# Dilated attention on one core: head pairs' products in runs, values stationary, one softmax scale, last group's values first

## The chip, the core and the metric

The kernel runs on one core of a Trainium2 chip. The metric is device time in microseconds (us), the median of three timed runs. A core has a matrix engine (TensorE, PE in the profile), a vector engine (VectorE, DVE), a scalar engine (ScalarE, ACT), a general engine (GpSimd, POOL), and a queue from which its transfers are issued (SyncE, SP). Each engine takes its own instructions in the order in which the program holds them, and waits on semaphores for the others.

## The reference, cut to what matters

Two layers act on 256 tokens of width 1024. Each is a gated feed-forward block, a mixer and another gated block, with RMS norms around each. The first layer's mixer is a convolution with a state-space part (the hybrid stage), the second's is the dilated attention that is changed here:

```python
qkv = (u @ w_qkv).reshape(bsz, seq, 3, ATTN_GROUPS, ATTN_HEADS, ATTN_HEAD_DIM)   # 3 groups, 8 heads, 64
for g, (window, dilation) in enumerate(DILATED_PATTERNS):
    o, l = dilated_window_attention(qkv[:, :, 0, g], qkv[:, :, 1, g], qkv[:, :, 2, g], slopes, window, dilation)
    outs.append(o)
    lses.append(l)
weights = jax.nn.softmax(jnp.stack(lses, axis=0), axis=0)
merged = jnp.einsum('gblh,gblhd->blhd', weights, jnp.stack(outs, axis=0).astype(jnp.float32))
return merged.reshape(bsz, seq, ATTN_OUT_WIDTH).astype(u.dtype) @ w_o
```

So there are three groups of eight heads, each with its own mask and its own softmax. The weighting over the groups by their log sums is the same as one softmax over the keys of all three groups together, and both kernels compute it in that way.

## The kernel before, in words

All activations stay on the chip; 178 weight units of 1 MB come in from memory. A product in nearly full f32 precision is made of three products of a rounded part (names `wh`, or `h`) and a rest (`wl`, or `l`). A weight unit lands in `raw`; ScalarE writes its rounded part `wh` and VectorE the rest `wl` in pieces of 128x1024 (`split`, `prefetch`). For units 38 to 55, those of the hybrid stage, GpSimd makes `wl` in pieces of 128x256. There are four slots each for `raw`, `wh` and `wl`.

The code does not fix the order of the instructions. Its functions record operations (`Recorder.add`), and `schedule` then places them: each engine takes, among the operations that could start at about the same estimated time, the one with the lowest rank, which is the order of recording with an offset from `moved`. The estimates come from `cost` and `latency`, and slots of buffers are given out in the same pass. All instructions are issued from line 423, so rows of the trace are told apart by tile names. `a`, `w`, `t` and `c` are PSUM banks (4, 2, 1 and 1 of them); `s` are the large SBUF slots (18), `cv`, `v`, `y` and `g` smaller kinds, `m` small columns, `x` the transposed input, `ident` the unit matrix.

Before the stage, the feed-forward stage hands over each half of the tokens (t = 0 and 1, 128 each) in turn: its last sums are normed and transposed into `x` (`_post_pre`, `to_transposed`). The attention stage is `attention`, line 1103:

- `values([0, 1])` multiplies the input by the value weights of groups 0 and 1, 24 matmuls for each token half and group, into a `w` bank (names `w<-wh,x`), and ScalarE copies the result to a `v` tile.
- For each group, `proj` makes q and then k, transposed (features on partitions), in `by_parts`: 16 matmuls into a `w` bank (names `w<-x,wh` and `w<-x,wl`), a ScalarE copy of one half, and a VectorE sum into a `cv` tile. One tile holds the four heads of two blocks; the even head of a pair lies on partitions 0 to 63, the odd one on 64 to 127.
- `softmax(g)` makes the scores. Half t = 0 has 128 keys and eight narrow products (64x128 by 64x128), half 1 has 256 keys and eight wide ones. They go to `a` banks. VectorE adds the mask table times the head's slope and takes the maxima, ScalarE exponentiates with the sums accumulated. From the second group on, the maximum is the running one, and factors `old` rescale the sums so far.
- `weigh(g)`, one group later, transposes the probabilities (72 transposes over all groups, into `t` and `c`), ScalarE copies them to `s` tiles, and 72 products with the probabilities stationary (128x128) and 64 columns of values moving give the weighted values, in an `a` bank. VectorE rescales the running sum `num` by `old` and adds.
- `values([2])` comes ahead of the last `weigh`. Then the sum is divided by the denominator, transposed (8 transposes), split, and multiplied by the output weights (48 matmuls, `a<-wh,x`), and the next stage's handover follows.

## Time and profile before

| | |
|---|---|
| timed runs | 1129.19, 1132.75, 1132.56 us; median 1132.56 |
| the profiled execution's own time | 1132.12 us, its span 1130.3 |
| TensorE busy | 1095.5 us of the span |
| VectorE, ScalarE, GpSimd busy | 738.6, 635.2, 148.2 us |
| granted TensorE clock, mean | 0.993 |
| attention stage on TensorE | 772.7 to 934.3 us of the span |
| hybrid stage | about 225 to 396 us |

The profile is of one execution. A row of a group of instructions reads: line, engine, operation, output <- inputs, partitions x elements, count, then busy time, mean length of one in ns, and idle time before them with what ended it. A row of the timeline begins with its start and length in us. A row of the sums by stretch gives the stretch, its length, and the busy time and number of instructions of PE, its weight loads, DVE, ACT and POOL, then granted clock, DMA share and GB/s. Matmuls overlap, so the time of a run is read from its start to the start of what follows; an f32 matmul leaves two records (two passes), each with a weight load of its own.

### The profile page before, as it was taken

What the parts mean: (1) busy time and instruction counts of PE and PEld (TensorE: products, weight loads), DVE (VectorE), ACT (ScalarE), POOL (GpSimd) and SP (SyncE); (2) the same over time, 40 slices, a digit from 0 to 9 for tenths busy, and PEclk for the clock granted to TensorE, in tenths of its full rate; (3) what the DMA queues carried; (4) which work ended last, traced back from release to release, by engine and by line L of the source; (5) the groups of instructions that cost most, each with busy time, mean ns of one, the idle gap of its engine ahead of it and who ended that gap; (6) DMA issues with size and microseconds to landing.
All of it is one profiled execution on the core that took longest, in us unless ns stands there. A gap on an engine that the chain in (4) does not pass through costs nothing.

```text
span 1130.3 us, 15336 instructions
## 1 busy us (share of the span) xinstructions
PE 1095.5 (97%) x5830; PEld 919.5 (81%) x5830; DVE 738.6 (65%) x1248; ACT 635.2 (56%) x1217; POOL 148.2 (13%) x200
## 2 busy tenths in 40 slices
PE   6999999999899999999999999999999999999997
PEld 5888888798767778888878888888877877888885
DVE  5756556799797685655686555667575657555563
ACT  7645545788667564554565454545565456455452
POOL 0000000379795300000010000001000000000000
PEclk9999999999999999999999999999999999999999
DMA  9755454534333466546546546554632424654521
GB/s 349 260 189 186 165 208 149 190 146 150 112 109 116 186 229 217 186 157 215 186 149 224 205 174 221 180 193 159 237 138 79 150 75 152 220 181 174 215 83 38
DMA packets 30203, 196.55 MB, mean 174 GB/s; under 512 B 3633, under 2 KB 4529, under 8 KB 7601
## 3 DMA queue, kind: packets, MB, share of 16 engines
q1 hardware_dynamic: 30128, 195.57, 48.9%
q8 instruction: 45, 0.74, 0.2%
q14 instruction: 30, 0.24, 0.1%
HBM read 194.51 MB, written 1.05 MB: 173 GB/s over the span
## 4 chain that ended last, share of the span: by engine, by line
PE 63%; DVE 4%; ACT 3%; POOL 3%; issue 1%; DVEq 0%; POOLq 0%; ACTq 0%
PE w L423 26%; PE a L423 22%; PE t L423 8%; PE c L423 7%; ACT s L423 1%; POOL wl L423 1%; ACT wh L423 1%; DVE y L423 1%; POOL s L423 1%; DVE wl L423 1%; DVE s L423 1%; POOL m L423 1%; DVE h L423 1%; DVE x L423 0%; DVE m L423 0%
## 5 line engine op out<-in xcount | busy, mean ns | idle before, releaser
L423 DVE TENSOR_TENSOR wl<-raw,wh 128x1024 fp32r<-128x1024 f32 (+1 forms) x322 | 385.1, 1220 | 215.6 <-ACT wh L423 214.0
L423 ACT ACTIVATE wh<-raw 128x1024 fp32r<-128x1024 f32 (+2 forms) x466 | 375.7, 854 | 232.4 <-PE a L423 91.5
L423 PE MATMUL w<-x,wh 128*128 128x512 f32 (+1 forms) x992 | 315.6, 373 | 3.5 <-DVE cv L423 2.1
L423 PE MATMUL w<-x,wl 128*128 128x256 f32 x880 | 247.9, 282 | 0.0
L423 PE MATMUL a<-wh,s 128*128 128x512 f32 x768 | 246.2, 395 | 0.0
L423 PEld LDWEIGHTS w<-x,wh 128*128 128x128 f32 x992 | 179.8, 189 | 40.2 <-DVE cv L423 3.1
L423 PEld LDWEIGHTS a<-wh,s 128*128 128x128 f32 x768 | 143.9, 188 | 34.7 <-DVE s L423 0.6
L423 PEld LDWEIGHTS w<-x,wl 128*128 128x128 f32 x880 | 166.9, 190 | 1.9 <-issue 0.6
L423 PE MATMUL w<-wh,x 128*128 128x512 f32 x480 | 159.3, 405 | 2.5 <-ACT x L423 2.5
L423 PE MATMUL a<-wl,s 128*128 128x512 f32 x384 | 151.8, 395 | 1.8 <-POOL wl L423 1.8
L423 POOL TENSOR_TENSOR m<-m,mhalf 128x1 f32<-128x1 f32 x28 | 19.6, 701 | 939.0 <-DVE m L423 939.0
L423 PEld LDWEIGHTS w<-wh,x 128*128 128x128 f32 x480 | 90.9, 191 | 24.6 <-ACT x L423 3.1
L423 POOL TENSOR_TENSOR wl<-raw,wh 128x256 fp32r<-128x256 f32 x144 | 103.7, 761 | 37.1 <-ACT wh L423 37.0
L423 PE MATMUL t<-x,wh 128*128 128x512 f32 x288 | 102.7, 396 | 0.0
L423 PE MATMUL c<-x,wh 128*128 128x512 f32 x288 | 102.7, 395 | 0.0
L423 PE MATMUL w<-wl,x 128*128 128x512 f32 x240 | 95.5, 400 | 1.7 <-POOL wl L423 1.7
L423 PEld LDWEIGHTS a<-wl,s 128*128 128x128 f32 x384 | 72.1, 188 | 17.6 <-POOL wl L423 2.2
L423 ACT ACTIVATE sg<-w 128x256 f32<-128x256 f32 x96 | 36.6, 382 | 86.7 <-PE w L423 86.6
L423 PE MATMUL t<-x,wl 128*128 128x256 f32 x288 | 80.8, 281 | 0.0
L423 PE MATMUL c<-x,wl 128*128 128x256 f32 x288 | 80.8, 281 | 0.0
L423 DVE TENSOR_TENSOR sg<-w,sg 128x256 f32<-128x256 f32 x72 | 30.3, 421 | 72.6 <-ACT sg L423 72.6
L423 PEld LDWEIGHTS t<-x,wh 128*128 128x128 f32 x288 | 54.0, 188 | 12.8
(167 smaller groups left out, 1211.3 us busy)
## 6 DMA issues: line engine op xcount, KB each, us to landing
raw<-in_weights SPq DMA_DIRECT2D x176, 1024.0 KB, 4.8
g<-in_gains SPq DMA_DIRECT2D x11, 512.0 KB, 4.7
raw<-in_weights SPq DMA_DIRECT2D x4, 256.0 KB, 6.1
raw<-in_weights SPq DMA_DIRECT2D x2, 512.0 KB, 7.9
out<-h SPq DMA_DIRECT2D x4, 256.0 KB, 2.1
s<-in_consts SPq DMA_DIRECT2D x3, 192.0 KB, 4.0
h<-in_x SPq DMA_DIRECT2D x2, 256.0 KB, 2.8
h<-in_x SPq DMA_DIRECT2D x1, 512.0 KB, 6.7
```

The lines of the kernel that those rows point to most:

```text
L423: o.ins = f(*[real(a) for a in o.args], **{k: real(a) for k, a in o.kw.items()})
```

## The change

Attention is recorded anew, and the estimates of two engines are altered.

- **Order of the weights.** The value weights of group 2 come first, then q and k of the three groups, then the values of groups 0 and 1 behind the last softmax. `values` makes one group at a time, with its copy hurried.
- **Banks.** q goes to the two `w` banks, k to `t` and `c` (before: both to `w`).
- **Runs.** A new context, `together`, gives its first operation the dependences of all operations in it, and the others a rank so low that they follow at once. The scores of an even and an odd head are issued in such runs, so that the two halves of the array's rows alternate; so are the products with the values.
- **Values stationary.** Of each weighted-value product the 64 columns of values now stand still, and the 128 columns of transposed probabilities move. The result comes out transposed, 64 partitions high: the even head of a pair on partitions 0 to 63, the odd one on 64 to 127, so that two heads use the two halves of the array's columns. All three groups add up in one bank for each token half (`po`).
- **One softmax scale.** Each group keeps its exponentials relative to the running maximum at its time. After the third group, `settle` forms a factor for groups 0 and 1 and GpSimd multiplies their twelve probability tiles (128x512) by it, broadcast along the keys; the denominator is summed once. `spread` writes the reciprocal wide, transposes it (8 transposes), and a single VectorE product per token half scales the result, which needs no transposing. Half of the transposed probabilities are copied by VectorE (`COPY`) where ScalarE copied all.
- **Slots.** The mask tables move from `s` to the two `g` slots, which they share with the gains of the handover. The probabilities of all three groups, 18 tiles, stay in `s`; their transposed copies go to `cv`.
- **Estimates.** `cost` has a lower price for products on half the array, and other prices for GpSimd. The latter alters the order in the hybrid stage, whose code is unchanged.

```diff
@@ _attn_units
-    out = []
-    for g in (0, 1):
-        out += _unit_a(sec(2, g))
+    out = _unit_a(sec(2, 2))
     for g in range(3):
         for s in (0, 1):
             c = sec(s, g)
             out += _unit_b(c[:, :256]) + _unit_b(c[:, 256:])
-    out += _unit_a(sec(2, 2))
+    for g in (0, 1):
+        out += _unit_a(sec(2, g))
@@ Recorder
+    @contextmanager
+    def together(self):
+        at = len(self.ops)
+        yield
+        head, rest = self.ops[at], self.ops[at + 1 :]
+        for o in rest:
+            for d, read in o.deps.items():
+                if d < at:
+                    head.deps[d] = head.deps.get(d, False) or read
...
+            o.rank = head.rank - RUN
+            o.deps.setdefault(o.index - 1, False)
@@ cost
+        if PAIRED and (stationary.ap.ap[0][1] == 64 or stationary.free_size() == 64):
+            return max(2 * n / 2.4 + 5.0, 110.0), 0.0
         return 2 * max(2 * n / 2.4 + 2.5, 112.0), 0.0
...
-        return (2.35 if out.ap.dtype == F32R else 1.9) * n + 40.0, 0.0
+        spread = any(isinstance(v, View) and v.ap.ap[-1][0] == 0 for v in kw.values())
+        return (1.95 if spread else 2.35) * n + (10.0 if spread else 92.0), 0.0
@@ attention
-                    by_parts(xT, unit, b, "w", o[:, b, :], scale)
+                    self.by_parts(xT, unit, b, banks[b], o[:, b, :], scale)
...
-            tabs = self.slot([P, 3 * P])
+            tabs = self.slot([P, 3 * P], tag="g")
...
+                    with nc.together():
+                        for j in range(per):
+                            b = i * per + j
+                            for r in range(2):
...
+                                nc.tensor.matmul(ps[r][:, j, :], q, k, start=True, stop=True)
...
+        def settle(t):
+            per = 4 // (t + 1)
+            den = sums[t][2]
+            for g in range(2):
+                f = self.sm(8)
+                V.tensor_tensor(out=f, in0=top[t][g], in1=top[t][2], op=ALU.subtract)
+                nc.scalar.activation(f, f, AF.Exp)
+                fv = f.rearrange("p (b r) -> p b r", r=2)
+                for n, s in enumerate(probs[t][g]):
+                    i, r = n // 2, n % 2
+                    nc.gpsimd.tensor_tensor(out=s, in0=s, in1=fv[:, i * per : (i + 1) * per, r].unsqueeze(2).to_broadcast([P, per, (t + 1) * P]), op=ALU.mult)
...
-                        nc.tensor.matmul(po[:, hd * 64 : (hd + 1) * 64], pT[idx // 4][:, idx % 4, :], vs[g][kb][:, hd * 64 : (hd + 1) * 64], start=kb == 0, stop=kb == nb - 1)
...
+            for i in range(0, 2 * nb, 2):
+                with nc.together():
+                    blocks = [divmod(n, nb) for n in range(4 * i, 4 * i + 8)]
+                    for kb in range(nb):
+                        for hd in sorted({hd for hd, _ in blocks}):
+                            n = hd * nb + kb
+                            out = po[t][(hd % 2) * 64 : (hd % 2) * 64 + 64, hd // 2, :]
+                            nc.tensor.matmul(out, v[kb][:, hd * 64 : (hd + 1) * 64], pT[n // 4][:, n % 4, :], start=g == 2 and kb == 0 and hd < 2, stop=g == 1 and kb == nb - 1 and hd >= 6)
...
+        v = values(2)
+        for g in range(3):
+            softmax(g, proj(0.125, "ww"), proj(1.0, "tc"))
+        rden = [settle(t) for t in range(NT)]
+        for t in range(NT):
+            weigh(2, t, v)
+        for g in range(2):
+            v = values(g)
             for t in range(NT):
+                weigh(g, t, v)
+            if g == 0:
+                rden = [spread(t, rden[t]) for t in range(NT)]
```

Three places of the order follow. First TensorE where the first weighted values stand. Before, these are group 0's, behind the projections of group 1; `a_7779` is the result of half 0, `v_7182` the values, `s_7661` and `s_7666` transposed probabilities, and `a_7808` and `a_7810` scores of group 1:

```order
L423 MATMUL a_7779<-v_7182,s_7661 128x64 x4
L423 MATMUL a_7779<-v_7182,s_7666 128x64 x4
L423 MATMUL t_7792<-ident_70,s_7552 128x128 x2
L423 MATMUL t_7792<-ident_70,s_7571 128x128 x2
L423 MATMUL c_7800<-ident_70,s_7552 128x128 x2
L423 MATMUL c_7800<-ident_70,s_7571 128x128 x2
L423 MATMUL a_7808<-cv_7711,cv_7617 128x128
L423 MATMUL a_7810<-cv_7711,cv_7617 128x128
L423 MATMUL a_7808<-cv_7711,cv_7617 128x128
L423 MATMUL t_7815<-ident_70,s_7579 128x128 x2
```

Now it is group 2, behind its softmax, and `w_8140` are value products of group 1 that stand between:

```order
L439 MATMUL a_8145<-cv_8135,v_7175 64x128 x4
L439 MATMUL a_8145<-cv_8098,v_7175 64x128 x4
L439 MATMUL t_8159<-ident_70,s_7967 128x128 x2
L439 MATMUL t_8159<-ident_70,s_7985 128x128 x2
L439 MATMUL w_8140<-wh_7907,x_7096 128x512 x2
L439 MATMUL w_8140<-wl_7927,x_7096 128x512
L439 MATMUL w_8140<-wh_7907,x_7096 128x512
L439 MATMUL w_8140<-wh_7907,x_7100 128x512
L439 MATMUL w_8140<-wl_7927,x_7100 128x512
L439 MATMUL t_8181<-ident_70,s_8027 128x128 x2
L439 MATMUL t_8181<-ident_70,s_8037 128x128 x2
L439 MATMUL a_8186<-cv_8172,v_7175 64x128 x2
```

The weighted values are 64 high and 128 wide where they were 128 high and 64 wide, in runs of eight, and value matmuls stand between the transposes where scores of the next group stood (three narrow products there stood apart from the rest of their group).

Second ScalarE at the first group's softmax. Before, from the end of the exponentials of half 0 (128x128) to those of half 1 (128x256), `cv_7617<-w_` being copies of projections:

```order
L423 ACTIVATE s_7527,m_2_7567<-s_7527,m_1_7561 128x128
L423 ACTIVATE s_7539,m_2_7567<-s_7539,m_1_7561 128x128
L423 ACTIVATE cv_7617<-w_7525 128x256
L423 ACTIVATE cv_7617<-w_7574 128x256
L423 ACTIVATE s_7552,m_5_7624<-s_7552,m_4_7620 128x256
L423 ACTIVATE s_7571,m_5_7624<-s_7571,m_4_7620 128x256
```

And now, the last of half 0's, the eight of half 1, and the copies:

```order
L439 ACTIVATE s_7476,m_2_7512<-s_7476,m_1_7507 128x128
L439 ACTIVATE s_7437,m_5_7560<-s_7437,m_4_7550 128x256
L439 ACTIVATE s_7457,m_5_7560<-s_7457,m_4_7550 128x256
L439 ACTIVATE s_7437,m_5_7560<-s_7437,m_4_7550 128x256
L439 ACTIVATE s_7457,m_5_7560<-s_7457,m_4_7550 128x256
L439 ACTIVATE s_7503,m_5_7560<-s_7503,m_4_7550 128x256
L439 ACTIVATE s_7514,m_5_7560<-s_7514,m_4_7550 128x256
L439 ACTIVATE s_7503,m_5_7560<-s_7503,m_4_7550 128x256
L439 ACTIVATE s_7514,m_5_7560<-s_7514,m_4_7550 128x256
L439 ACTIVATE cv_7495<-w_7492 128x256
L439 ACTIVATE cv_7597<-w_7534 128x256
L439 ACTIVATE cv_7602<-t_7522 128x256
```

The copies of the second and third q bank and of the first k bank have moved behind all sixteen exponentials; the copy of the first q bank stands ahead of them.

Third GpSimd in the hybrid stage, where it splits weights (`wl`) and multiplies the state-space inputs. Before:

```order
L423 TENSOR_TENSOR wl_2782<-raw_2498,wh_2736 128x256 x8
L423 TENSOR_TENSOR wl_2860<-raw_2577,wh_2822 128x256 x5
L423 TENSOR_TENSOR s_2908<-v_2891,m_5_2150 128x512
L423 TENSOR_TENSOR s_2924<-v_2897,m_5_2150 128x512
L423 TENSOR_TENSOR v_2891<-v_2891,heads_122 128x512
L423 TENSOR_TENSOR v_2897<-v_2897,heads_122 128x512
L423 TENSOR_TENSOR wl_2860<-raw_2577,wh_2822 128x256 x3
```

And now:

```order
L439 TENSOR_TENSOR wl_2744<-raw_2431,wh_2576 128x256 x8
L439 TENSOR_TENSOR wl_2831<-raw_2514,wh_2731 128x256 x7
L439 TENSOR_TENSOR s_2900<-v_2882,m_5_2150 128x512
L439 TENSOR_TENSOR s_2918<-v_2887,m_5_2150 128x512
L439 TENSOR_TENSOR v_2882<-v_2882,heads_122 128x512
L439 TENSOR_TENSOR v_2887<-v_2887,heads_122 128x512
L439 TENSOR_TENSOR wl_2831<-raw_2514,wh_2731 128x256
```

Seven pieces of the unit stand ahead of the four products where five did.

## The prediction

> **What bounds the kernel now.** I read the page first. Its first part says that TensorE (PE) works nearly without a break, its clock row that the throttle gives it full speed.

> ```profile
> span 1130.3 us, 15336 instructions
> PE 1095.5 (97%) x5830; PEld 919.5 (81%) x5830; DVE 738.6 (65%) x1248; ACT 635.2 (56%) x1217; POOL 148.2 (13%) x200
> PEclk9999999999999999999999999999999999999999
> ```

> So a change helps by what it takes off PE's own time, and harms by each wait it puts there. Next, the timeline of PE (start, length, engine, operation, count, and in brackets the idle time before it) gives the stage's borders: its first value product starts at 772.67, its last output product ends at 934.2. The sums by stretch show PE idle for 161.60 - 155.63 = 6.0 us there, 2.0 of it in the last 23 us.

> ```profile
> 772.67 0.40 PE L423 MATMUL w<-wh,x 128*128 128x512 f32 x1
> 780.71 0.63 PE L423 MATMUL t<-ident,y 128*128 128x128 f32 x4 [0.21 <-DVE y L423]
> 781.53 0.48 PE L423 MATMUL w<-wh,x 128*128 128x512 f32 x1
> 772.70:934.30 161.60, 155.63 (x906) 130.45 (x905) 102.12 (x196) 92.32 (x217) 3.04 (x4) 0.99 0.41 145
> 911.30:934.30 23.00, 20.95 (x130) 17.51 (x129) 14.44 (x23) 12.65 (x27) 1.09 (x2) 1.00 0.27 92
> ```

> Last, who PE waits for (in total, times, longest), first in this stage, then in the hybrid stage (225 to 396), whose order also moves:

> ```profile
> PE w L423 <- DVE cv L423: 2.1, 1, 2.1
> PE t L423 <- ACT s L423: 1.3, 2, 1.0
> PE a L423 <- DVE cv L423: 0.9, 1, 0.9
> PE a L423 <- DVE s L423: 0.7, 3, 0.3
> ...
> PE a L423 <- POOL wl L423: 4.6, 2, 2.8
> PE w L423 <- POOL wl L423: 1.7, 1, 1.7
> PE a L423 <- POOL s L423: 0.8, 1, 0.8
> ```

> The projections, the value and output products and the 72 transposes of probabilities keep their number, so only what follows counts.

> **Weighted values (probabilities by values).** Grouped by shape, and one run of them with the row behind it:

> ```profile
> L423 PE MATMUL a<-v,s 128*128 128x64 f32 x144 | 16.7, 273 | 0.0
> 848.27 1.90 PE L423 MATMUL a<-v,s 128*128 128x64 f32 x16
> 850.00 0.61 PE L423 MATMUL t<-ident,s 128*128 128x128 f32 x4
> ```

> 72 products leave 144 records (an f32 product is two passes). A run of 16 takes 850.00 - 848.27 = 1.73, so 0.108 a pass, and all of them 144 x 0.108 = 15.6 us. Now the values stand still in 64 columns, and 128 columns of probabilities move: twice the columns a pass. Nothing in this trace is a column pair. The nearest rows are the scores, whose even and odd heads take the two halves of the array's rows:

> ```profile
> L423 PE MATMUL a<-cv,cv 64*128 64x256 f32 x48 | 9.9, 398 | 0.7 <-DVE s L423 0.7
> L423 PE MATMUL a<-cv,cv 64*128 64x128 f32 x48 | 4.5, 297 | 0.9 <-DVE cv L423 0.9
> 818.91 1.80 PE L423 MATMUL a<-cv,cv 64*128 64x128 f32 x20
> 856.25 2.92 PE L423 MATMUL a<-cv,cv 64*128 64x128 f32 x22
> ```

> The order of before has six narrow and four wide products at the row of 818.91, so twelve and eight passes. One after another at the 0.108 of a 128-column pass (0.215 for 256, twice that) they would take 12 x 0.108 + 8 x 0.215 = 3.0; side by side in twos 1.5. It took 1.80, so the pairs do run together, and 0.28 goes for starting and emptying a run. If column pairs behave so, 72 products take 144 x 0.108 / 2 = 7.8, plus nine runs of 0.28 = 2.5, together 10.3: **-5.3 us**. Bounds: -7.8 without a run's 0.28, and +2.5 if no pair forms (15.6 + 2.5). I take -5.3, because the nearest rows pair.

> [...]

> **Scores.** The row of 856.25 shows what a broken order costs: ten narrow and twelve wide passes (five and six products), paired 1.8 by the same prices, took 2.92. The two groups above are 9.9 + 4.5 busy and 1.6 of waiting, 16.0 in all. Issued as three runs a group (four wide, eight narrow, four wide products): 3 x (8 x 0.108 + 8 x 0.215 + 3 x 0.28) = 10.3, **-5.7 us**; the waits go, since a run waits as a whole, behind other matmuls. If 1.6 of waiting stays, -4.1.

> **Projections.** q keeps the two w banks and k gets t and c, so PE can be four projections ahead of the copies instead of two: the 2.1 us wait for DVE cv goes, **-2.1** (nothing if ACT holds the copies back; see the rivals).

> **The stage's start.** Values of one group, not two, stand ahead of the other token half's transposes. Before, 33 products filled 772.67 to 780.71, 0.244 each; now 24 fill 5.9 of these 8.0 us, and nothing else is ready: 2.2 of idle time. Then the second half's products need the low parts of x:

> ```profile
> 780.88 2.35 DVE L423 TENSOR_TENSOR wl<-raw,wh 128x1024 fp32r<-128x1024 f32 x2
> 783.15 0.75 DVE L423 TENSOR_TENSOR x<-t,x 128x256 fp32r<-128x256 f32 x2
> ```

> Before, 15 products covered that. Now one of the two splits stands ahead, so the parts come about 1.1 earlier, near 782.5, and PE waits some 0.6 more. **+2.8 us** (2 to 4).

> **Softmax scale and the end.** The per-group rescaling on VectorE (DVE) goes; it was off PE's path, worth nothing. In its place GpSimd (POOL) multiplies the twelve tiles of groups 0 and 1, in one row:

> ```profile
> L423 POOL TENSOR_TENSOR s<-s,m 128x512 f32<-128x512 f32 x2 | 2.1, 1066 | 0.0
> L423 POOL TENSOR_TENSOR wl<-raw,wh 128x256 fp32r<-128x256 f32 x144 | 103.7, 761 | 37.1 <-ACT wh L423 37.0
> 370.74 5.07 POOL L423 TENSOR_TENSOR wl<-raw,wh 128x256 fp32r<-128x256 f32 x3
> 371.80 3.43 DVE L423 TENSOR_TENSOR wl<-raw,wh 128x1024 fp32r<-128x1024 f32 x2
> L423 DVE TENSOR_REDUCE m<-s 128x2 f32<-128x512 f32 x12 | 8.2, 680 | 0.0
> L423 DVE SCALAR_TENSOR_TENSOR s<-s,a 128x256 f32<-128x256 f32 x24 | 9.2, 414 | 0.0
> L423 DVE SCALAR_TENSOR_TENSOR s<-s,a 128x128 f32<-128x128 f32 x24 | 5.2, 280 | 5.2 <-PE a L423 5.2
> L423 ACT ACTIVATE s<-s,m 128x128 f32<-128x128 f32 x24 | 9.3, 389 | 3.8 <-DVE m L423 3.8
> L423 ACT ACTIVATE s<-s,m 128x256 f32<-128x256 f32 x24 | 11.8, 497 | 0.0
> ```

> Count from the first score of group 2. DVE needs 8 x 0.28 + 8 x 0.41 + 6 x 0.68 = 9.6 for biases and maxima, two thirds of it until half 0's are known (about 7 with the wait for PE). ACT then has 8 x 0.39 and 8 x 0.50 = 7.1 of exponentials and the scale's own behind them: GpSimd starts near +15.5. Group 0's second half needs its first eight products, 8 x 1.07 = 8.6: +24. PE arrives there after 61 matmuls at 0.233 (14.2), 28 transposes at 0.11 (3.1), the scores (3.4) and two runs of weighted values (2.3), +23, and uses the last of the eight at about +24.4. No slack, then; and GpSimd beside a DVE split ran at 5.07 / 3 = 1.69 for 0.76. Two or three splits fall into that time, 0.93 each: **+2.0** (0 to 5). Group 1's products come some 14 us later on PE and are covered. Eight transposes issued singly among matmuls, another **+0.5**. The last part still has 24 transposes going through one t and one c bank with nothing to fill in; I leave its 2.0 idle as it is (0 to 4).

> SyncE's queue: the three tables take the slots of the gains, so the next gains wait for softmax 1 and 2, and weights queue behind them. The weights are split several units ahead of PE, so I cost that at nothing; without that cover it would be one landing, about 5.

> **The hybrid stage** gets another order only because GpSimd's costs are re-estimated. PE waits 4.6 + 1.7 + 0.8 = 7.1 for GpSimd there, 2.8 of it at one place, for the splits of a weight unit of which five stood ahead of four products and three behind them. Now seven stand ahead (the order's third place), which takes most of that wait; but GpSimd's work is no shorter, and something behind the four products can come late instead: **-2.0**, between -5 and +2.

> **Sum.** -5.3 - 5.7 - 2.1 + 2.8 + 2.0 + 0.5 - 2.0 = -9.8. The profiled execution took 1132.1 (1.8 outside its span; the median of the three timed runs is 1132.6, so it stands for them): **1122.3 us**.

> **Rivals.**
> No column pairs: 7.8 more, 1130.1. For it: no row shows one; the change would then not do what it says. Against: row pairs do, and even and odd heads alternate in the new order. [...]

> GpSimd late (the 2.0 grows to 5 and the tail to 4): 1127.3. [...]

> Slower than before, by one mechanism: ACT now runs all sixteen exponentials of a group, 7.1 us, ahead of the copy of the second w bank, where two copies stood between them. PE needs that bank at +17.4 (scores 3.4, then 79 products at 0.177, as 128 took 818.91 - 796.23); it is free near +15.5. From 2 us of lateness on DVE or ACT each microsecond is PE's; it happens after groups 0 and 1. If the whole run lies bare, 2 x 7.1 = 14.2, 1136.5. For it: the maxima wait behind splits on DVE. Against: ACT stood 3.8 us waiting for these maxima in before (the row above), and PE's wait for DVE cv was 2.1 in all.

> ```profile
> 796.23 0.40 PE L423 MATMUL w<-x,wh 128*128 128x512 f32 x1
> ```

> Better than forecast: the hybrid's waits mostly go (-5 for -2) and a column run empties for nothing (-2.5): 1116.8.

> **How the numbers follow.** Forecast 0.52 (its own terms give 1117 to 1127), slowed pairs 0.06, no pairs 0.11, GpSimd late 0.10, slower 0.09, better 0.12. The range 1113 to 1133 leaves out the slower case and the far end of the better one, under 2 in 10. A measurement here tells 0.3% (3.4 us) from no change: faster, below 1129.2, takes the forecast, the slowed pairs, the better case and 0.06 of GpSimd late, 0.76; the same takes 0.09 of "no pairs" and 0.04 of GpSimd late, 0.13; slower takes the rest, 0.11.

> **What would show it.** Weighted values as a form of 64 columns, 144 records, each run of 16 near 1.15 us: right; near 1.7 to 2: no pairs. Scores about 10 us with no wait inside a run. One idle of about 2 us ahead of the transposes at the stage's start. PE's wait for "POOL s" near 2; PE's wait for DVE cv gone, or, if the slower case holds, 5 us and more in it. Waits for "POOL wl" in the hybrid stage near 4, the single one of 2.8 gone. The forecast is wrong if the attention stage is not 5 to 10 us shorter, or if more than 5 us of the change comes from outside it.

## The result, and the profile after

The changed kernel takes 1115.34 us (median of 4 runs, 1115.06 to 1115.64) where the kernel before took 1131.97 beside it (4 runs): a ratio of 0.9857, with an interval of 0.984 to 0.9875. It is faster by 16.6 us. The forecast was 1122.3 with a range of 1113 to 1133: the direction and the range held, but the gain is 7 us larger than the sum had it.

The profile's first part, its span and its busy row. The span is 16.7 us shorter, and PE's busy time 11.2:

```profile
span 1113.6 us, 15360 instructions
PE 1084.3 (97%) x5830; PEld 906.9 (81%) x5830; DVE 744.7 (67%) x1249; ACT 632.3 (57%) x1210; POOL 162.6 (15%) x212
```

The sums by stretch: the attention stage's opening up to its first projection, its last section, and the whole stage from its first value product to the end of its last output product. The number behind POOL's is the granted clock:

```profile
768.90:785.40 16.50, 14.21 (x58) 10.71 (x57) 13.00 (x23) 9.08 (x17) 1.94 (x2) 0.90 0.63 215
899.80:919.60 19.80, 18.12 (x122) 14.02 (x120) 12.59 (x22) 10.09 (x22) 1.10 (x2) 1.00 0.31 107
768.90:919.60 150.70, 146.73 (x906) 118.50 (x904) 108.07 (x197) 89.08 (x210) 17.13 (x16) 0.99 0.46 158
```

The stage is 150.7 long where it was 161.6. Between the two stretches, from 785.4 to 899.8, PE does not stand still at all: what idle time the stage has is 2.3 at the start and 1.7 at the end. And in the opening the clock is 0.90.

PE's timeline at the three runs of scores of one group and at a run of weighted values, each with the row behind it:

```profile
808.05 1.14 PE L439 MATMUL a<-cv,cv 64*128 64x256 f32 x8
809.12 0.50 PE L439 MATMUL w<-x,wh 128*128 128x512 f32 x1
...
810.58 1.16 PE L439 MATMUL a<-cv,cv 64*128 64x128 f32 x16
811.67 0.39 PE L439 MATMUL w<-x,wl 128*128 128x256 f32 x1
812.22 1.14 PE L439 MATMUL a<-cv,cv 64*128 64x256 f32 x8
813.28 0.38 PE L439 MATMUL w<-x,wl 128*128 128x256 f32 x1
...
877.54 1.09 PE L439 MATMUL a<-cv,v 128*64 128x128 f32 x16
878.57 0.66 PE L439 MATMUL t<-ident,s 128*128 128x128 f32 x4
```

A run of sixteen passes of weighted values takes 878.57 - 877.54 = 1.03, against 1.73 before and 1.15 in the forecast. The scores of a group take 1.07 + 1.09 + 1.06 = 3.2.

Who PE waits for, in the attention stage and then in the hybrid stage:

```profile
PE t L439 <- DVE y L439: 2.4, 2, 2.3
PE c L439 <- DVE cv L439: 0.9, 1, 0.9
PE t L439 <- ACT cv L439: 0.6, 1, 0.6
...
PE w L439 <- POOL wl L439: 3.2, 1, 3.2
PE w L439 <- ACT v L439: 2.5, 1, 2.5
PE a L439 <- POOL wl L439: 1.3, 1, 1.3
```

The wait for a `w` bank of projections (DVE cv, 2.1) is gone (0.9 for DVE cv stands ahead of a transpose's `c` bank), and there is none for GpSimd's products (POOL s). In the hybrid stage PE waits 4.5 for the splits, where it waited 6.3. The single wait of 2.8 ahead of an `a` bank is gone, and the one ahead of a `w` bank has grown from 1.7 to 3.2.

The next table splits the stage by what PE works on: the time from the start of each matmul to the start of the next, summed by kind over the trace, with the idle time ahead of a kind beside it. "Forecast" is the term of the prediction.

| us, elapsed + idle | before | after | difference | forecast |
|---|---|---|---|---|
| weighted values | 15.95 | 9.21 | -6.74 | -5.3 |
| scores | 13.54 + 1.57 | 9.67 | -5.44 | -5.7 |
| projections | 70.15 + 2.14 | 68.45 | -3.84 | -2.1 |
| transposes | 10.69 + 1.77 | 9.90 + 3.93 | +1.37 | +2.2 start, +0.5 lone ones, +2.0 GpSimd |
| value products | 33.72 | 37.86 + 0.03 | +4.17 | +0.6 |
| output products | 11.56 + 0.48 | 11.62 | -0.42 | 0 |
| stage | 161.57 | 150.67 | -10.90 | -7.8 |

Outside the stage the span lost another 5.8. Set against the start of the same matmul in before, PE is 0.9 earlier ahead of the hybrid stage (no changed instruction has run by then: 0.2 come from the first loads, 0.7 from the granted clock, whose first stretch at 1.00 begins at 13.9 us of the span here and at 16.0 in before: there the starts of 128x512 products go from 0.43 apart to 0.23), gains 2.4 in the hybrid stage, 0.5 in the two feed-forward stages behind it, 1.0 in the last one, and 1.0 between the last matmul and the end.

### The profile page after: what moved, and what is told of

Its sections match the earlier page's. It is cut to its first block, busy times and chain, and to the rows that moved or that the text cites. A ratio compares the mean times of both kernels' runs of the same rounds, so it can differ in the third digit from the quotient of the medians.

```text
span 1113.6 us, 15360 instructions
## 1 busy us (share of the span) xinstructions
PE 1084.3 (97%) x5830; PEld 906.9 (81%) x5830; DVE 744.7 (67%) x1249; ACT 632.3 (57%) x1210; POOL 162.6 (15%) x212
## 4 chain that ended last, share of the span: by engine, by line
PE 86%; DVE 6%; ACT 3%; POOL 2%; issue 1%; DMA 1%; SPq 0%; DVEq 0%; POOLq 0%; ACTq 0%
PE w L439 33%; PE a L439 30%; PE t L439 12%; PE c L439 11%; DVE c L439 1%; POOL wl L439 1%; ACT wh L439 1%; DVE t L439 1%; DVE y L439 1%; DVE wl L439 1%; DVE h L439 1%; POOL m L439 1%; DVE x L439 1%; DMA gain<-in_chan 1%; DVE s L439 0%
## 5 line engine op out<-in xcount | busy, mean ns | idle before, releaser
L439 PE MATMUL w<-x,wh 128*128 128x512 f32 (+1 forms) x896 | 279.4, 368 | 1.2 <-DVE pt L439 0.8
L439 PE MATMUL a<-wh,s 128*128 128x512 f32 x800 | 256.5, 395 | 0.0
L439 PE MATMUL w<-x,wl 128*128 128x256 f32 x784 | 220.6, 281 | 0.0
L439 PEld LDWEIGHTS w<-x,wh 128*128 128x128 f32 x896 | 160.8, 188 | 31.9 <-issue 1.4
L439 PEld LDWEIGHTS w<-x,wl 128*128 128x128 f32 x784 | 147.9, 189 | 2.6 <-issue 0.9
L439 PE MATMUL t<-x,wh 128*128 128x512 f32 x336 | 119.2, 394 | 0.0
L439 PE MATMUL c<-x,wh 128*128 128x512 f32 x336 | 119.1, 394 | 0.0
L439 PE MATMUL t<-x,wl 128*128 128x256 f32 x336 | 94.1, 280 | 0.0
L439 PE MATMUL c<-x,wl 128*128 128x256 f32 x336 | 94.1, 280 | 0.0
L439 PEld LDWEIGHTS c<-x,wh 128*128 128x128 f32 x336 | 63.0, 188 | 14.6 <-DVE cv L439 0.2
```

Of the source, the lines that this page charges most:

```text
L439: o.ins = f(*[real(a) for a in o.args], **{k: real(a) for k, a in o.kw.items()})
```

## The experiments

All ratios are against the kernel before, run beside each kernel on the same chip; its medians were 1131.97, 1132.71, 1131.80 and 1131.76.

| kernel | us | ratio, interval |
|---|---|---|
| changed | 1115.34 | 0.9857, 0.984 to 0.9875 |
| 1 heads apart | 1118.37 | 0.9878, 0.9863 to 0.9893 |
| 2 former GpSimd price | 1119.53 | 0.9885, 0.9868 to 0.9901 |
| 3 scores without runs | 1118.88 | 0.9879, 0.9865 to 0.9894 |
| 4 start filled | 1113.88 | 0.9837, 0.9823 to 0.9852 |
| 5 two groups' values first | 1119.00 | 0.9892, 0.9875 to 0.9909 |
| 6 k to the w banks | 1124.85 | 0.9937, 0.9924 to 0.9949 |
| 7 before, new GpSimd price | 1126.68 | 0.9957, 0.9944 to 0.997 |
| 8 start and hybrid waits filled | 1112.16 | 0.9828, 0.9815 to 0.9842 |
| 9 GpSimd later | 1122.06 | 0.9913, 0.99 to 0.9927 |
| 10 start filled, low parts last | 1111.48 | 0.9818, 0.9805 to 0.9832 |

The theory going in: the gain is that two products run side by side, in column pairs and row pairs, and what the sum missed is the clock. In the trace of after, the granted clock stands at 0.5 for 3.41 us behind the wait at the stage's start; in before, behind the wait for a projection's bank.

### 1. Heads apart

```diff
-                    for kb in range(nb):
-                        for hd in sorted({hd for hd, _ in blocks}):
+                    for hd in sorted({hd for hd, _ in blocks}, key=lambda h: (h % 2, h)):
+                        for kb in range(nb):
```

> The changed kernel, with the products of each run of weighted values issued all even heads first, then all odd ones, so that neighbours use the same half of the array's columns (but for one border a run). Numbers, shapes, banks and runs stay. Theory (the gain of the weighted values is column pairs running side by side): each run of 16 records grows from 1.03 us to between 1.7 and 1.9, nine runs +6 to +8, time about 1122 us. Rival (the gain comes from values being stationary, 64 columns to load and 128 to move, whoever the neighbour is): runs stay near 1.03 us, time within 1 us of 1115.3.

PE's timeline at the first run, and the row behind it:

```profile
877.83 1.58 PE L439 MATMUL a<-cv,v 128*64 128x128 f32 x16
879.34 0.66 PE L439 MATMUL t<-ident,s 128*128 128x128 f32 x4
```

Each of the nine runs takes 1.51 in place of 1.03; the nine together 13.59 for 9.21, +4.4. The attention stage is 4.0 longer in the profiled execution, which is the longest of the four (1120.03 us); the median is up by 3.0, the ratio by 0.0021 (2.4 us). So the gain is the pairs. The loss is less than expected most likely because pairs still form around the border, where the odd heads follow the even ones. An estimate with the 0.109 of a pass: 4 single, 4 double and 4 single passes are 1.31, and 0.2 for starting and emptying makes the 1.5 that the run takes. In after, the records of a run start in twos, 0.01 apart, a pair every 0.109: a pair takes as long as one pass alone (the 128x128 transposes at 15.23 us of the span of after start 0.109 apart, one by one). Two f32 products on the two halves of the array's columns lose nothing here, a factor of 2.0 inside the run.

### 2. The former price of GpSimd's products

```diff
-        spread = any(isinstance(v, View) and v.ap.ap[-1][0] == 0 for v in kw.values())
-        return (1.95 if spread else 2.35) * n + (10.0 if spread else 92.0), 0.0
+        return (2.35 if out.ap.dtype == F32R else 1.9) * n + 40.0, 0.0
```

> The changed kernel with the former price of GpSimd's products, which gives the hybrid stage its former order back. Theory (the hybrid stage's share of the gain is its order): TensorE's waits for GpSimd there go back from about 4.5 to about 7 us, with the single one of 2.8, and the stage is 2.5 us longer, time about 1117.8 us. Rival (the stage's share is drift from one execution to the next): the order changes, the stage's length stays, time within 0.7 us of 1115.3.

The waits of the hybrid stage are those of before again:

```profile
PE a L439 <- POOL wl L439: 4.6, 2, 2.7
PE w L439 <- ACT v L439: 2.4, 1, 2.4
PE w L439 <- POOL wl L439: 1.7, 1, 1.7
```

The time is up by 4.2 us (0.0028 in the ratio, 3.2 us), more than the theory's 2.5. Against kernel 1, which is the same up to attention but for this order, PE loses 3.2 in the hybrid stage, 0.7 more in the two feed-forward stages behind it and 0.6 in the last. The order carries the stage's share, and the small drift of unchanged stages goes with it; why those matmuls run 0.2 to 0.3 per cent slower was not found.

### 3. Scores without runs

```diff
-                    with nc.together():
+                    if True:
```

> The changed kernel with the scores recorded without runs: per group six narrow and four wide products, seven matmuls of other work, two narrow, two others, two wide, two others, two wide, where the changed kernel has four wide, seven others, eight narrow, two others, four wide. Theory (the gain of the scores is that each run starts and empties at 0.28 us and waits once): one more stretch in each group and single waits come back, +1 to +2.5 us, time 1116.5 to 1118, scores 11 to 12 us. Rival A (only whole runs pair): scores go back to some 15 us, time about 1120.5. Rival B (the runs are worth nothing, the gain came from banks and from the order of groups): scores stay near 9.7 us, time within 0.7 us of 1115.3.

The timeline of the first group's last two pieces, and the row behind the first:

```profile
812.21 1.13 PE L439 MATMUL a<-cv,cv 64*128 64x256 f32 x4
813.27 0.38 PE L439 MATMUL w<-x,wl 128*128 128x256 f32 x1
...
813.82 1.13 PE L439 MATMUL a<-cv,cv 64*128 64x256 f32 x4
```

Two wide products take 1.06, twice, as much as four in a run of after (1.07): four passes one after the other (4 x 0.215 and 0.2), where those of a pair start 0.01 apart in after. Most likely the scheduler put two of the same parity together, which share their rows; the trace doesn't name the heads. All scores take 12.8 us, +3.1, and the time is up by 3.5 us (2.5 by the ratios); scores and median lie above the theory's ranges. That is over half of what the runs brought (5.4 with the waits). No single wait came back. The three extra stretches cost about 0.2 each and not 0.28; the rest, some 2.5, is what the theory left out: a free order also parts the pairs.

### 4. The start filled

```diff
+FILL = 20
...
+                if g == 2 and t == 0:
+                    idle = self.ps([P, 512], "a")
+                    for k in range(FILL):
+                        x = self.xa(xT, 0, k % KB)[0]
+                        nc.tensor.matmul(idle[:, 0:P], x, x, start=True, stop=True)
```

> The changed kernel with 20 unused matmuls (128x128, from the transposed input of the first token half into a bank that nobody reads) recorded at the stage's start; 16 of them stand in the gap ahead of the second half's transposes. They add work and take no wait away. Theory (an idle time of TensorE of about 2.2 us is followed by 3.4 us at half the granted clock): with the gap filled the clock stays at 1.0, the 24 value products of the second half take about 5.6 us in place of 7.35, and the time falls by about 1.7 us less 0.5 for the four dummies outside the gap, about 1114.0 us. Rival (the 7.35 us are waiting for the low parts of the input): the products still take over 7 us, time 1115.3 to 1116.

Sums by stretch over the wait and the 3.41 us behind it, first of after, then of this kernel:

```profile
775.08:778.50 3.42, 1.53 (x10) 1.15 (x10) 2.98 (x5) 1.14 (x5) 1.18 (x1) 1.00 0.67 184
778.50:781.91 3.41, 3.41 (x9) 2.48 (x8) 2.34 (x5) 0.31 (x2) 0.00 (x0) 0.50 0.46 190
```

```profile
775.42:778.83 3.41, 2.90 (x28) 2.78 (x26) 2.97 (x5) 1.06 (x3) 1.40 (x1) 1.00 0.50 127
778.83:782.24 3.41, 3.41 (x18) 2.61 (x17) 2.78 (x6) 0.80 (x4) 0.00 (x0) 1.00 0.58 243
```

The clock stays at 1.00. The 24 value products take 5.77 (779.00 to 784.77) in place of 7.35, and the kernel with more work in it is 1.5 us faster, 1113.88 (2.3 by the ratios). The clock theory holds, the low parts of x are no part of it.

### 5. The values of two groups first

```diff
-    out = _unit_a(sec(2, 2))
+    out = _unit_a(sec(2, 2)) + _unit_a(sec(2, 0))
...
-        v = values(2)
+        v = values((2, 0))
...
+        v.update(values((1,)))
```

> The changed kernel with the values of two groups (2 and 0) ahead of the second token half's transposes at the stage's start, as the kernel before had two there, and only group 1's behind the last softmax. The number of matmuls stays. Theory (the start's idle time of 2.25 and its 3.4 us at half clock are worth 4.0 us, and the value products at the other end cover little): no idle time and full clock at the start, -4.0; at the end the transposes of one group and a half lose their cover and wait 0.3 to 0.5 each for one t and one c bank, +1 to +2; together about 1113 us. Rival (those value products are the cover of the last section): some 24 transposes more go bare and wait, +4 to +8, one wait of over 2.1 us bringing a stretch of half clock, together 1115 to 1120.

Sums by stretch of the opening and of the last section, then PE's longest waits in the stage:

```profile
768.90:785.40 16.50, 16.34 (x75) 13.07 (x74) 11.48 (x22) 8.81 (x18) 1.94 (x2) 1.00 0.63 215
896.00:922.70 26.70, 22.89 (x169) 17.35 (x167) 15.17 (x25) 9.98 (x23) 2.56 (x3) 1.00 0.23 79
```

```profile
PE t L438 <- ACT cv L438: 3.0, 4, 1.1
PE c L438 <- DVE cv L438: 2.6, 3, 1.8
PE a L438 <- ACT s L438: 1.2, 1, 1.2
```

The start is as it was expected, 0.16 idle in 16.5 and a clock of 1.00. But the waits at the other end sum to 6.8 (1.5 in after), the stage is 3.2 longer than after's, and the time 3.7 (4.0 by the ratios). So the rival has it: the value products of two groups are worth more as cover for the transposes than ahead of the start. The change's order of the values pays its 3.9 at the start for a good reason.

### 6. k to the w banks

```diff
-            softmax(g, proj(0.125, "ww"), proj(1.0, "tc"))
+            softmax(g, proj(0.125, "ww"), proj(1.0, "ww"))
```

> The changed kernel with k sent to the two w banks again, as q. Theory (the banks t and c took away the waiting for the copies, and one wait of 2.1 us cost 3.8 with its stretch of half clock): TensorE waits again for ACT or DVE ahead of projections, at the places where the exponentials of a group stand ahead of the copies, 2 us and more at one or two of them, each with 3.4 us at half clock: +3.8 to +8, 1119 to 1123 us. Rival (the wait went with the order of groups and the runs, not with the banks): no such wait, within 0.7 us of 1115.3.

PE's waits ahead of a projection's `w` bank in the stage, in total, times, longest:

```profile
PE w L439 <- DVE cv L439: 5.3, 3, 3.7
```

One wait is 3.66 long, and 3.41 at half clock follow it; the stage is 158.94 long, +8.3, of which 5.4 are waits and 1.7 the clock. The time is up by 9.5 us (9.1 by the ratios), the largest step of all and above the theory's 8. Ahead of the long wait ScalarE begins a group's sixteen exponentials at 816.12 and copies the next bank at 823.15, right behind the last of them; VectorE's sum waits 3.38 for that copy, and PE for the sum. So the exponentials ahead of the copies do hold back the banks, as the prediction's slower rival said, and t and c are what keeps this away from PE.

### 7. The kernel before with the new price

The diff is that of the second experiment the other way round, in the kernel before.

> The kernel before with nothing but the new price of GpSimd's products, so the hybrid stage gets its new order and attention stays as it was. Theory (the order is worth in the kernel before what it is worth in the changed one, where the former price cost 3.7 us up to the attention stage): -3.7 us, about 1129. Rival (the gain needs the rest of the change): within 1 us of 1132.5.

The time falls by 5.1 us, more than expected. Of the 6.2 between the two spans 1.2 lie ahead of the hybrid stage (0.5 of loads, 0.7 of the clock, which is at 1.00 from 14.0 us here), 2.1 in it, 1.2 in unchanged feed-forward stages, and 1.65 in the attention stage, whose instructions are those of before. There the wait for the bank is the same (2.09 for 2.14), but the clock is not. The window of 3.41 us that holds that wait in before and the one behind it, and then three windows here:

```profile
869.29:872.70 3.41, 1.27 (x10) 0.98 (x9) 0.95 (x4) 3.41 (x14) 0.00 (x0) 1.00 0.00 0
872.70:876.11 3.41, 3.41 (x12) 2.91 (x12) 1.23 (x1) 1.15 (x2) 0.00 (x0) 0.51 0.02 2
```

```profile
863.90:867.32 3.42, 2.24 (x16) 1.83 (x14) 1.45 (x3) 3.42 (x16) 0.00 (x0) 1.00 0.00 0
867.32:870.73 3.41, 2.50 (x14) 2.19 (x15) 1.73 (x4) 2.57 (x7) 0.00 (x0) 1.00 0.00 0
870.73:874.14 3.41, 3.41 (x21) 2.92 (x20) 2.23 (x4) 2.28 (x3) 0.00 (x0) 1.00 0.58 175
```

In before the wait lies within one window and leaves it 1.27 busy; here a border of windows cuts it into 1.18 and 0.91, and no stretch at half clock follows. Projections take 68.61 here and 70.15 in before. So it is not the length of a wait alone that decides, as the expectation for the eighth kernel has it (from about 2.1 us up), but also where it falls.

### 8. The hybrid stage's waits filled

On top of the filled start, the program's issue puts unused matmuls ahead of two waiting instructions, the 11th product into `w` bank buffer 40 and the first transpose into buffer 44:

```diff
+IDLE = {("w", 40, 10): (7, ("a", 35)), ("w", 44, 0): (4, ("a", 36))}
...
+                    times, bank = IDLE.get((*key, n), (0, None))
...
+                        for _ in range(times):
+                            self.tc.nc.tensor.matmul(real(to), real(xs[0]), real(xs[1]), start=True, stop=True)
```

> The kernel with the filled start, and unused matmuls at two more places: 7 of 128x512 ahead of the hybrid stage's wait of 3.2 us for GpSimd, and 4 ahead of its wait of 2.5 us for ScalarE, which leaves 1.6 us of idle time at each. What PE waits for comes no sooner. Theory (an idle time from about 2.1 us up brings 3.4 us at half clock, one of under 1.9 does not): both stretches of half clock go, -1.7 to -3.4 us against the filled start's 1113.9, so 1110.5 to 1112.2. Rival A (the clock falls after a certain share of idle time in a longer stretch, whatever a single wait's length): the stretches stay, 0. Rival B (the stretches go, but the next wait takes the time back): within 0.7 us of 1113.9.

The window with each wait and the one behind it:

```profile
327.42:330.83 3.41, 1.71 (x7) 1.07 (x7) 3.41 (x11) 0.00 (x0) 3.41 (x6) 1.00 0.26 53
330.83:334.24 3.41, 3.41 (x16) 2.82 (x15) 3.41 (x11) 0.93 (x3) 3.41 (x6) 1.00 0.98 408
...
337.66:341.07 3.41, 1.75 (x12) 1.06 (x10) 2.97 (x8) 3.41 (x9) 3.41 (x5) 1.00 0.56 235
341.07:344.48 3.41, 3.19 (x17) 2.09 (x14) 2.79 (x11) 3.41 (x13) 2.68 (x5) 1.00 0.01 2
```

PE is idle for 1.70 and 1.66 of these windows and the clock is 1.00 in all four. The hybrid stage is 1.7 shorter than in kernel 4, the time 1.7 (1.0 by the ratios, whose intervals overlap): the theory's lower end. That the stretches go is shown by the windows; the time alone would not part the theory from rival B. PE gains 1.6 behind the first wait and only 0.3 behind the second, where the transposes that ran at half clock are followed by a wait for their copies (ACT x, 0.22 here).

### 9. GpSimd later

```diff
+                if t == 0 and g == 0:
+                    spare = self.slot([P, per, (t + 1) * P], BF16, "junk")
+                    for _ in range(4):
+                        nc.gpsimd.tensor_tensor(out=spare, in0=probs[t][g][0], in1=..., op=ALU.mult)
+                        nc.ops[-1].cost = 0.0
```

> The changed kernel with four unused products of 128x512 on GpSimd ahead of the first of the twelve multiplications, so all twelve come about 4.2 us later; the order on the other engines stays. Theory (GpSimd was early by a margin: the sixth, seventh and eighth product were done 1.1, 1.5 and 1.2 us before TensorE's transposes used them): TensorE now waits 4.2 - 1.1 = 3.1 us in all for POOL s, and if a single wait fills more than half of a 3.4 us window, a stretch of half clock comes on top, 1.7: 1118.4 to 1120.1 us. Rival (these products are off the path by more than 4 us, as the absence of any wait might suggest): within 0.7 us of 1115.3.

GpSimd's products in after, then here, with PE's wait for them and the windows around its long part:

```profile
876.54 14.09 POOL L439 TENSOR_TENSOR s<-s,m 128x512 f32<-128x512 f32 x12 [100.28 <-ACT m L439]
```

```profile
880.63 13.08 POOL L439 TENSOR_TENSOR s<-s,m 128x512 f32<-128x512 f32 x12
```

```profile
PE t L439 <- POOL s L439: 3.4, 3, 2.6
```

```profile
882.85:886.26 3.41, 1.37 (x7) 0.84 (x7) 1.10 (x2) 0.60 (x1) 3.41 (x3) 1.00 0.00 0
886.26:889.68 3.42, 2.58 (x8) 1.90 (x9) 0.00 (x0) 0.60 (x1) 3.42 (x4) 0.50 0.00 0
889.68:893.09 3.41, 3.41 (x23) 2.55 (x22) 0.00 (x0) 0.00 (x0) 3.41 (x5) 0.50 0.00 0
893.09:896.50 3.41, 3.41 (x26) 2.72 (x26) 2.96 (x3) 1.20 (x2) 0.63 (x1) 1.00 0.19 24
```

The products come 4.1 later. PE waits 3.4 for them (3.1 expected), and two windows run at half clock where the theory had one: +6.7 us (6.3 by the ratios), beyond the theory's 1120.1, and the stage is 6.3 longer. In after GpSimd was early by little more than 1 us, and that was all there was between no wait and 6 us.

### 10. The start filled, low parts last

```diff
+    def lo_last(self, ps, xT, t, units):
...
+        for kb, (hi, lo), k in at:
+            x = self.xa(xT, t, kb)
+            mm(ps, x[0], hi[:, k, :], start=kb == 0, stop=False)
+            mm(ps, x[1], hi[:, k, :], start=False, stop=False)
+        for kb, (hi, lo), k in at:
+            mm(ps, self.xa(xT, t, kb)[0], lo[:, k, :], start=False, stop=kb == KB - 1)
...
-                self.tok_major(ps, xT, t, unit)
+                self.lo_last(ps, xT, t, unit)
```

> The kernel with the filled start, and in the hybrid stage's gate products the eight matmuls with the weights' low parts behind the sixteen with the rounded parts, in place of one after every two; the same products in another order of adding up. Theory (the stage's wait of 3.2 us is for GpSimd's low parts alone): the low parts are wanted up to 16 matmuls of 0.23 later, so the wait of 3.2 goes, with its stretch of half clock if no other wait takes its place: -3.2 to -4.9 us against the filled start's 1113.9, so 1109 to 1110.7. Rival (the stage is bound by VectorE's and ScalarE's chain to the gate's second token half, so TensorE only waits somewhere else): the wait for ScalarE grows by what is saved, within 0.7 us of 1113.9.

The hybrid stage's longest waits:

```profile
PE w L439 <- ACT v L439: 4.7, 1, 4.7
PE w L439 <- ACT y L439: 1.3, 1, 1.3
```

The waits for GpSimd's splits are gone, and the wait for ScalarE behind them has grown from 2.5 to 4.7. The clock is low behind it: the seven transposes there take 1.76, where the eight behind the wait of 1.3 take 1.14. The profile's mean clock is 0.996 where kernel 8 has 0.999, by an estimate two stretches of 3.41 us at half clock. Up to the stage's output products (`a<-wh,s`) 0.8 is left of the gain, near what the rival had; 1.2 more come at their start, where the last of the waits for splits (1.3 in after) is gone too, and 0.9 in the two unchanged feed-forward stages behind. The medians differ by 2.4 us from kernel 4 (2.2 by the ratios), between theory and rival. At 1111.48 us this is the lowest median of all, though its interval overlaps kernel 8's, and 20 of its matmuls do nothing but fill the start's gap.

## Why the prediction was right, and where it was wrong

By its own test the forecast was wrong at the edge: it allowed 5 to 10 us in the attention stage and 5 outside, and the runs gave 10.9 and 5.8. The mechanisms of the gain were the right ones; several terms were mis-sized, and the clock was not in the sum. Part of the surplus is luck as far as the prediction goes: the 0.9 ahead of any changed instruction, and the 1.7 at half clock behind the bank's wait in before (see Projections), both hang on where the clock's changes fell in the two profiled executions.

**Weighted values** (-5.3, measured -6.7). Pairs form, as the row pairs of the scores had suggested. A run takes 1.03 and not 1.15, since starting and emptying costs 0.16 and not 0.28, and the former runs took 15.95 and not 15.6. The 0.28 came from the length of a row, 1.80, whose last record overlaps with what follows: in after the next matmul starts 0.06 to 0.08 ahead of the end of such a row, which leaves about 1.73 of the 1.80 (an estimate). The rival "no pairs" falls with the first experiment. That two products of a pair slow each other, which has 0.06 among the chances, no run shows: a pair took 0.109, as a pass alone.

**Scores** (-5.7, measured -5.4). Right to 0.3, no wait inside a run. That it is so close is luck: the same overlapping tails were in the 16.0 of before (15.1 from start to start) and in the 10.3 forecast (9.7 measured), and the two cancel.

**Projections** (-2.1, measured -3.8). The wait of 2.14 went as forecast. The rest, 1.7, is the stretch at half clock behind it: the prediction read the page's clock row, whose tenths hide a stretch of 3.4 in a slice of 28 us. It is owed to the position of that wait in the profiled execution: in kernel 7 the same wait costs 2.1.

**The stage's start** (+2.8, measured +3.9). 2.25 of idle time where 2.2 was forecast. The further 0.6 for the low parts of x did not come, 1.7 at half clock came instead; the fourth experiment parts the two.

**GpSimd** (+2.0, measured 0). The step that failed is PE's arrival. The count from the first score of group 2 had GpSimd starting at +15.5 and PE using the last of its eight products at +24.4; they came at 876.54 - 860.27 = +16.3 and at 887.0 - 860.27 = +26.7. The eighth product was done at +25.4: only one of the eight met a DVE split (2.10 against 1.04) where two or three were put in. PE came later because from the first score to there 65 value products took 17.0, 0.26 each, where 61 at 0.233 (14.2) were counted. The ninth experiment shows how near that was. The last section's idle time, left at 2.0, came to 1.7, and no wait of PE for a transfer appeared in the stage, as forecast for SyncE's queue.

**Lone transposes** (+0.5). Value products, beyond the 1.7 of the clock, take 2.5 more and transposes 0.8 less: a value product behind a transpose or a run takes 0.31 to 0.34 in place of 0.23 (one takes 0.43). That is +1.7 for work that now stands in small pieces, a term three times the one forecast; it is also what delays PE under GpSimd.

**The slower rival** (16 exponentials hold back the copies) did not come, as PE had four banks for the projections; the sixth experiment shows its mechanism at work as soon as there are two.

**Hybrid stage** (-2.0, measured -2.4). GpSimd waits of 4.5 against "near 4"; the single one of 2.8 went, and a later one, ahead of a `w` bank, grew from 1.7 to 3.2: something behind the four products came late instead, as the term's range allowed. By experiments 2 and 7 the order is worth 2.1 to 3.2 there and 1.2 to 1.3 more in stages that it does not touch. **Outside**: of the -0.9 ahead of any changed instruction 0.2 is the landing of the first loads and 0.7 the earlier full clock. The last 1.0 lies between the last matmul and the end, which takes 7.3 us in before and 6.2 in after: the last output transfer lands 3.1 us after its issue in before and 2.0 in after. Why it does stays open.

## What to carry to other kernels

Two products on the two halves of the array's columns, or rows, ran here at the price of one (0.109 us a pair, 0.109 a pass alone) where neighbours in the order alternated. Issuing the whole group as a run keeps a scheduler from parting the pairs, and saves about 0.2 us for each stretch less. Where PE is bound, read each wait together with the clock behind it: the wait at the stage's start in after and the one for a projection's bank in before left PE idle for 1.9 and 2.1 us of one of the clock's windows (next section), and each cost its own length and about 1.7 us more; where the wait went or was filled, in after and in kernel 4, so did the stretch at half clock. And before moving cover from one place to another, price the place that loses it: the value products at the end of the stage were worth more than the 3.9 us at its start (experiment 5).

## What the runs showed of the hardware

The grid's place differs between executions (16.0 and 13.9 above, 14.0 in kernel 7), and the same wait of 2.1 or 2.5 us was followed by 3.41 us at half clock in one and not in another: that of 2.1 in before but not in kernel 7, and that of 2.5 for ACT v in after, where it left 1.96 idle in one window, but not in kernel 6, where a border of windows cut it (1.61 us idle in the first, and the clock at 1.00 in the second). The timed runs agree: of the nine of the kernel before that stand beside kernels 9 and 10, the shortest took 1129.92 us at a mean granted clock of 0.995 and the longest 1133.49 at 0.992, and 0.003 of the mean clock is two windows at half clock, 3.4 us. So a difference of 1.7 us between two profiled executions can be the grid's alone.
